# Forget-gate attention: half-row scores of two heads, token-major values, and an order written out for five engines

## The chip, the cores and the metric

The kernel runs on one core of a Trainium2 chip. The metric is the time on the device of one execution, in microseconds (us). Of the core's engines the text speaks of PE (TensorE: matmuls and transposes; its weight loads are recorded apart, as PEld), DVE (VectorE), ACT (ScalarE), POOL (GpSimd) and SP (SyncE, which issues most of the transfers).

## What is computed

The program is two transformer blocks over 1024 tokens of width 1024. All of the change lies in one layer of the first block, the forget-gate attention ("fox"): 16 heads of 64, a causal softmax over scores to which the difference of two cumulative log forget gates is added.

```python
def fox_layer(x, g_in, w_in, b_f, w_out):
    h = rms_norm(x, g_in)
    z = h @ w_in
    q, k, v, f_logit, gate = split_cols(z, ODD_SPLITS)     # 1024, 1024, 1024, 16, 1024
    log_f = jax.nn.log_sigmoid(f_logit.astype(jnp.float32) + b_f.astype(jnp.float32))
    log_cum = jnp.cumsum(log_f, axis=1)
    o = causal_block_attention(q.reshape(B, S, FOX_HEADS, FOX_HEAD_DIM), ..., log_cum=log_cum)
    return x + (o.reshape(B, S, FOX_WIDTH) * jax.nn.silu(gate)) @ w_out

# causal_block_attention, for each block of 128 queries:
        s = jnp.einsum('bqhd,bkhd->bhqk', qi, k) * scale
        s = s + ci[..., :, None] - lc_t[..., None, :]
        s = jnp.where(kpos[None, :] <= qpos[:, None], s, -jnp.inf)
        p = jax.nn.softmax(s, axis=-1)
        o = jnp.einsum('bhqk,bkhd->bqhd', p, v)
```

Products of single precision are made of three matmuls on operands that are split into a high and a low part (`mm3`: high by high, high by low, low by high).

## The kernel before

**Rounds.** The 16 heads are taken as 8 pairs p, and each pair runs over 8 query blocks i: 64 rounds n = 8p + i. In round n the scores are (i+1)·128 keys wide. `pipeline` with `FOX_SKEW = [2, 1, -2]` makes step t out of four things: scores and softmax of round t+2 (`soft`), the transposes of the probabilities of round t+1 (`tr`), the product with the values of round t-2 (`pv`), and `fill(t)`, which is one half of a projection of the next pair: 24 matmuls of 512 columns and their evacuation. Pairs 0 and 1 have three projections (q, k, gate), the pairs from 2 on also v: 8 units. In the last pair's steps `fill` runs units of a later stage (`k.mem.fill`) and loads for the layer's output projection (`ahead`).

**Scores.** For one head the high half of q stands on 64 partitions of a tile and the low half on the other 64, and the keys' high part (another tile: their low part) stands twice, on both halves. So a head's scores are two matmuls over all 128 rows (L595). The copies of the keys into the other half are 64 transfers of 128 KB issued by ACT (L1256, L1257), and q and k are evacuated by two instructions on 64 partitions for each part (L1245, L1246, L1254, L1255). DVE adds the bias and finds the row's bound (L600, two instructions or three for a head, the last one on the diagonal block with `dm` of L1309 on POOL), ACT makes the exponentials and their sum (L606), DVE the reciprocal (L608), POOL the scaling (L609).

**Transposes and values.** `tr` transposes up to four 128x128 blocks into one of two `pt` banks (L622), and ACT copies the bank out (L630): for i of 4 and more there are four such groups in a round, two for each head. `pv` multiplies with the values of the two heads, 64 output rows each, the heads one after the other (L644). The values of pairs 0 and 1 are made token by token ahead of the rounds (`V01`); those of the pairs from 2 on come out of a projection as features by tokens and are transposed back, 8 transposes for each pair (L1276) with two copies on DVE (L1277).

**Order.** In this stage SP alone issues in the source's order. PE, DVE, ACT and POOL are ordered by the scheduler, and the four generators of a step hand over to each other at each `yield`; a few order-only dependencies (`k.order`) keep transposes, products and projections of neighbouring rounds apart.

**Weights.** `plan` puts every weight piece on one list. `w_get` (used by `proj_units`) splits a piece into high and low (a cast on ACT, L316, a subtraction on DVE, L318) and also the next one on the list, one ahead, unless that one is marked `slot`.

PSUM has 8 banks here: two `pd` (projections), three `ps` (scores), two `pt` (transposes), one `po` (products).

## Time and profile before

| | us |
|---|---|
| median of three runs (lowest, highest) | 2300.29 (2298.59, 2302.42) |
| the profiled execution, its own time | 2301.81 |
| its span in the trace | 2300.0 |
| PE busy in the span | 2211.1 (96%) |
| rounds of the fox layer, 608.0 to 1203.2 | 595.2 |
| PE busy in them | 591.9 |
| DVE, ACT, POOL busy in them | 258.1, 274.6, 154.9 |

The page puts a core's engines side by side. The chain of waits follows the work that ended last back from the end of the program. A view by form groups instructions of one line and one shape with their mean duration; consecutive matmuls overlap in their records, so what one adds on PE is the distance between two starts, which the timeline gives. The view by windows gives each engine's busy time and the granted clock of PE in a stretch.

### The profile page before, as it was taken

The page shows a single profiled execution, that of the slowest core. Times are in us where ns is not written, and L with a number is a line of the kernel's source. Part 1 is how long each engine was busy: PE and PEld are TensorE (multiplying, and loading weights), DVE is VectorE, ACT ScalarE, POOL GpSimd, SP SyncE. Part 2 cuts the span into 40 slices and gives each one's busy share as a digit, 9 for nine tenths or more (in the row PEclk, how much of TensorE's full clock was granted, in tenths as well). Part 3 has the DMA queues.
Part 4 walks back from the last instruction along what each step waited for, and adds up shares of the span by engine and source line. Part 5 has one row for each costly group of instructions (what it writes and reads, how often), then busy time and mean ns, then how long its engine had stood idle before and what let it go on. Part 6 is the DMA issues. An engine that isn't in the chain of part 4 may idle for free.

```text
span 2300.0 us, 32867 instructions
## 1 busy us (share of the span) xinstructions
PE 2211.1 (96%) x12164; PEld 1757.5 (76%) x12164; DVE 1184.4 (51%) x2892; ACT 960.0 (42%) x2018; POOL 452.6 (20%) x620
## 2 busy tenths in 40 slices
PE   7999999999999999999999999999899999899797
PEld 7888778888877777777788789787577888666564
DVE  6322678834344443444344332687445637766544
ACT  5322667823344444444442221355202122557453
POOL 2000455400122222222310010121001102222121
PEclk9999999999999999999999999999999999999898
DMA  4112221233222211221254221326656124778774
GB/s 165 37 48 99 81 58 38 75 118 104 75 69 72 63 55 60 74 60 56 83 174 147 103 91 47 106 69 216 233 220 259 69 106 176 263 235 293 226 216 165
DMA packets 96515, 282.06 MB, mean 123 GB/s; under 512 B 11980, under 2 KB 25036, under 8 KB 96352
## 3 DMA queue, kind: packets, MB, share of 16 engines
q1 hardware_dynamic: 75616, 225.32, 28.4%
q0 software_dynamic: 6624, 24.12, 4.4%
q10 hardware_dynamic: 14112, 30.48, 4.2%
q8 instruction: 97, 1.59, 0.3%
q14 instruction: 66, 0.54, 0.1%
HBM read 202.73 MB, written 65.62 MB: 117 GB/s over the span
## 4 chain that ended last, share of the span: by engine, by line
PE 85%; DVE 6%; DMA 4%; ACT 3%; issue 2%; SPq 0%; POOL 0%; ACTq 0%; POOLq 0%; DVEq 0%
PE pd L340 15%; PE pd L342 15%; PE pd L341 15%; PE ps L340 4%; PE po L644 4%; PE ps L342 4%; PE ps L341 4%; PE ps L595 3%; PE pt L622 3%; PE pd L2538 2%; PE pd L1902 2%; PE ps L990 2%; PE po L1033 1%; PE pt L1019 1%; PE ps L2562 1%
## 5 line engine op out<-in xcount | busy, mean ns | idle before, releaser
L340 PE MATMUL pd<-fh,wh 128*128 128x512 f32 x880 | 353.5, 402 | 0.6 <-DVE st L1246 0.3
L342 PE MATMUL pd<-fh,wl 128*128 128x512 f32 x880 | 347.9, 395 | 0.5 <-DVE wl L318 0.5
L341 PE MATMUL pd<-fl,wh 128*128 128x512 f32 x880 | 347.4, 395 | 0.0
L340 PE MATMUL pd<-wh,fh 128*128 128x258 f32 (+3 forms) x616 | 203.2, 330 | 2.4 <-DVE n L1436 2.4
L342 PE MATMUL pd<-wh,fl 128*128 128x258 f32 (+3 forms) x616 | 200.9, 326 | 0.0
L341 PE MATMUL pd<-wl,fh 128*128 128x258 f32 (+3 forms) x616 | 200.8, 326 | 0.0
L340 PEld LDWEIGHTS pd<-fh,wh 128*128 128x128 f32 x880 | 165.2, 188 | 43.0 <-issue 7.1
L342 PEld LDWEIGHTS pd<-fh,wl 128*128 128x128 f32 x880 | 165.2, 188 | 40.1 <-issue 2.3
L341 PEld LDWEIGHTS pd<-fl,wh 128*128 128x128 f32 x880 | 165.5, 188 | 34.9 <-issue 0.2
L318 DVE TENSOR_TENSOR wl<-w,wh 128x1024 fp32r<-128x1024 f32 (+5 forms) x92 | 106.8, 1166 | 138.3 <-ACT wh L316 138.3
L316 ACT CAST wh<-w 128x1024 fp32r<-128x1024 f32 (+5 forms) x99 | 97.3, 989 | 139.3 <-PE pd L341 108.2
L630 ACT COPY PT<-pt 128x512 f32<-128x512 f32 (+2 forms) x192 | 86.4, 478 | 139.9 <-PE pt L622 139.4
L609 POOL TENSOR_SCALAR P<-P,rinv 128x256 f32<-128x256 f32 (+7 forms) x128 | 96.1, 751 | 192.3 <-DVE rinv L608 163.3
L606 ACT ACTIVATE P<-P,m 128x256 f32<-128x256 f32 (+7 forms) x128 | 99.6, 778 | 76.7 <-DVE m L600 75.8
L340 PEld LDWEIGHTS pd<-wh,fh 128*128 128x128 f32 x616 | 116.4, 189 | 14.2 <-DVE n L1436 2.8
L341 PEld LDWEIGHTS pd<-wl,fh 128*128 128x128 f32 x616 | 116.3, 189 | 10.6 <-issue 1.0
L342 PEld LDWEIGHTS pd<-wh,fl 128*128 128x128 f32 x616 | 116.3, 189 | 10.2 <-issue 0.2
L1309 POOL TENSOR_TENSOR dm<-lcb,mask 128x128 f32<-128x128 f32 x128 | 60.7, 474 | 282.4 <-DVE m L600 226.3
L595 PE MATMUL ps<-st,st 128*128 128x512 f32 (+3 forms) x384 | 106.9, 372 | 1.2 <-DMA st<-st 0.8
L644 PE MATMUL po<-PT,V 128*64 128x256 f32 (+1 forms) x640 | 96.4, 373 | 0.0
L2420 DVE TENSOR_TENSOR ml<-mw,mh 128x1024 fp32r<-128x1024 f32 x66 | 80.1, 1226 | 29.8 <-ACT mh L2417 15.4
L622 PE MATMUL pt<-ident,P 128*128 128x128 f32 x576 | 88.7, 276 | 2.6 <-POOL P L609 2.4
(513 smaller groups left out, 4721.9 us busy)
## 6 DMA issues: line engine op xcount, KB each, us to landing
mw<-w_moe SPq DMA_DIRECT2D x70, 512.0 KB
w<-o_wc SPq DMA_DIRECT2D x30, 512.0 KB
w<-w_moe SPq DMA_DIRECT2D x26, 512.0 KB
xr<-xs SPq DMA_DIRECT2D x18, 512.0 KB
s<-x_wkv SPq DMA_DIRECT2D x16, 512.0 KB
lcb<-dn SPq DMA_DIRECT2D x16, 512.0 KB
st<-st ACTq DMA_DIRECT2D x64, 128.0 KB
wkd<-kvw SPq DMA_DIRECT2D x32, 256.0 KB
```

The lines of the kernel that those rows point to most:

```text
L316: nc.scalar.copy(hi[:, :n], raw[:, :n])
L318: (eng or nc.vector).tensor_sub(lo[:, :n], raw[:, :n], hi[:, :n].bitcast(F32))
L340: first = mm(out, lhs[0], rhs[0], start=start, stop=False)
L341: mm(out, lhs[0], rhs[1], start=False, stop=False)
L342: mm(out, lhs[1], rhs[0], start=False, stop=stop)
L595: ins = nc.tensor.matmul(ps[:, :m], l, r, start=t == 0, stop=t == len(passes) - 1)
L606: nc.scalar.activation(sb[:, :w], sb[:, :w], AF.Exp, bias=acc, scale=-1.0, accum_out=sm)
L609: nc.gpsimd.tensor_scalar(sb[:, :w], sb[:, :w], ri, 0.0, op0=OP.mult, op1=OP.add)
L622: ins = nc.tensor.transpose(pt[:, j * 128:(j + 1) * 128], p[:, (c + j) * 128:(c + j + 1) * 128], k.ident)
L630: nc.scalar.copy(dst, src)
L644: st["V", n + i] = nc.tensor.matmul(o[a * 64:(a + 1) * 64, cols], val(a, j), PT[i // 2, a, j // 4][:, j % 4, n0:], start=j == 0, stop=j == ...
L2420: nc.vector.tensor_sub(W[c][1], raw[c], W[c][0].bitcast(F32))
```

## The change

The scores of both heads of a pair are made together. q and k are kept as four tiles (q high, q low, k high, k low), each with head 0 on partitions 0 to 63 and head 1 on 64 to 127; three matmuls for each head, over 64 rows each, alternate between the heads and go to separate banks. The copies of the keys go away, and each half of q or k is evacuated by one ACT and one DVE instruction on 128 partitions.

The values of two pairs (256 columns) are made token by token, in units of two token blocks: 48 matmuls 256 columns wide, 12 units for six pairs, at i = 6 and 7 of pairs 0 to 5. The transposes of the values go away. Their weights (`o_wv2`, two `slot` pieces for two pairs) stand in the list behind the pieces of pairs 1, 3 and 5, and are split in step i = 4 of pairs 0, 2 and 4.

The generators become plain functions, and all five engines issue in the source's order: `outs`, `score`, `turn`, `soft`, `fill` in each step.

```diff
+FOX_MAN = {ET.SP, ET.PE, ET.DVE, ET.Activation, ET.Pool}
...
+    A["o_wv2"] = np.stack([v[:, c * 256:(c + 1) * 256].reshape(8, 128, 256).transpose(1, 0, 2).reshape(128, 2048) for c in range(1, 4)])
...
-        ch += [q[:, c], kk[:, c]] + ([v[:, c]] if p >= 2 else []) + [gate[:, c]]
+        ch += [q[:, c], kk[:, c], gate[:, c]]
...
-def causal_attn(k, st, n, qk, bias, scale, val, done):
...
         def q_evac(half, ps):
...
-                nc.scalar.activation(q[r, cols], ps[r, :], AF.Copy, scale=0.125)
...
+            h, l = qk[p][:2]
+            nc.scalar.activation(h[:, cols], ps, AF.Copy, scale=0.125)
+            nc.vector.scalar_tensor_tensor(l[:, cols], ps, 0.125, h[:, cols].bitcast(F32), op0=OP.mult, op1=OP.subtract)
...
-                k.q.dma_start(out=h[o, cols].bitcast(F32), in_=h[r, cols].bitcast(F32))
-                k.q.dma_start(out=l[o, cols].bitcast(F32), in_=l[r, cols].bitcast(F32))
+            h, l = qk[p][2:]
+            nc.scalar.copy(h[:, cols], ps)
+            nc.vector.tensor_sub(l[:, cols], ps, h[:, cols].bitcast(F32))
...
+    def v_weights(g):
+        WV[g] = [k.w_get(i, 0) for i in k.fv2[g]]
+
+    def v_unit(g, x):
+
+        if x % 2 == 0:
+            V.setdefault(g, []).append(k.slot([128, 4, 256], name="V"))
+        ps = k.psd()
+        for t in range(2):
+            for kt in range(8):
+                wh, wl = WV[g][kt // 4]
+                c = slice(kt % 4 * 256, (kt % 4 + 1) * 256)
+                k.mm3(ps[:, t * 256:(t + 1) * 256], ft.stat(2 * x + t, kt), (wh[:, c], wl[:, c]), kt == 0, kt == 7)
+        nc.scalar.copy(V[g][x // 2][:, x % 2 * 2:x % 2 * 2 + 2, :].rearrange("p a b -> p (a b)"), ps)
...
+    def score(n):
+
+        p, i = divmod(n, 8)
+        w = (i + 1) * 128
+        qh, ql, kh, kl = qk[p]
+        ps = {}
+        for c in range(0, w, 512):
+            m = min(512, w - c)
+            for a in range(2):
+                ps[c, a] = k.psd() if c and a else k.pss()
+            for l, r in ((qh, kh), (qh, kl), (ql, kh)):
+                for a in range(2):
+                    h = slice(a * 64, a * 64 + 64)
+                    nc.tensor.matmul(ps[c, a][:, :m], l[h, i * 128:w], r[h, c:c + m], start=l is qh and r is kh, stop=l is ql)
...
+    def turn(n):
+        i, z = n % 8, n // 2
+        for a in range(2):
+            p = P.pop((n, a))
+            for c in range(0, i + 1, 4):
...
+                pt = k.pst()
+                for j in range(m):
+                    nc.tensor.transpose(pt[:, j * 128:(j + 1) * 128], p[:, (c + j) * 128:(c + j + 1) * 128], k.ident)
...
     def fill(t):
         p, i = divmod(t, 8)
...
         if i == 0:
             units[p] = prep(p + 1)
-        if i >= len(units[p]):
-            return []
...
+            g = p // 2 + 1
+            if p < 6:
+                units[p] += [lambda x=x: v_unit(g, x + p % 2 * 2) for x in range(2)]
+                if p % 2 == 0:
+                    units[p][4] = lambda u=units[p][4]: (u(), v_weights(g))
+        if i < len(units[p]):
             units[p][i]()
...
-    pipeline(64, [run(0), run(1), run(2)], FOX_SKEW, fill)
...
+    a, b, c = FOX_SKEW
+    with k.tc.manual_schedule(engines=FOX_MAN):
+        for t in range(-a, 64 - c):
+            if 0 <= t + c:
+                outs(t + c)
+            if t + a < 64:
+                score(t + a)
+            if 0 <= t + b < 64:
+                turn(t + b)
+            if t + a < 64:
+                soft(t + a)
+            if t < 64:
+                fill(t)
+            else:
+                weave([ahead(t - 56)])
...
+        k.fc.append([k.plan(A["o_wc"][p * 3 + j]) for j in range(3)])
+        if p in (1, 3, 5):
+            k.fv2[p // 2 + 1] = [k.plan(A["o_wv2"][p // 2, :, b * 1024:(b + 1) * 1024], 1024, True) for b in range(2)]
```

The next rows are PE's order before, at the transposes of block 5 of pair 3's first head (`pt` banks), with scores of block 6 (`ps`) and a projection (`pd`):

```order
L341 MATMUL pd_8801<-fl_5423,wh_8515 128x512
L342 MATMUL pd_8801<-fh_5422,wl_8516 128x512
L595 MATMUL ps_8755<-st_7657,st_7655 128x512 [waits DVE_49,PE_49]
L622 MATMUL pt_8693<-ident,P_8590 128x128 [waits Activation_49,Pool_49]
L622 MATMUL pt_8693<-ident,P_8590 128x128 x3
L622 MATMUL pt_8750<-ident,P_8590 128x128 [waits Activation_49]
L622 MATMUL pt_8750<-ident,P_8590 128x128
L595 MATMUL ps_8755<-st_7659,st_7655 128x512
L340 MATMUL pd_8801<-fh_5422,wh_8515 128x512
L595 MATMUL ps_8766<-st_7657,st_7655 128x384 [waits DVE_49]
L595 MATMUL ps_8766<-st_7659,st_7655 128x384
L341 MATMUL pd_8801<-fl_5423,wh_8515 128x512
```

The two groups of the second head follow 22 rows further down, behind the rest of that projection. The same place of the change, one block further (block 6 of pair 3, with the end of the scores ahead of it):

```order
L1230 MATMUL pd_8988<-qk_7823,qk_7821 128x512
L1230 MATMUL ps_8987<-qk_7823,qk_7822 128x512
L1230 MATMUL pd_8988<-qk_7823,qk_7822 128x512
L1265 MATMUL pt_9014<-ident,P_8890 128x128 [waits Pool_49]
L1265 MATMUL pt_9014<-ident,P_8890 128x128 x3
L1265 MATMUL pt_9021<-ident,P_8890 128x128 [waits Activation_49]
L1265 MATMUL pt_9021<-ident,P_8890 128x128 x2
L1265 MATMUL pt_9027<-ident,P_8899 128x128 [waits Activation_49,Pool_49]
L1265 MATMUL pt_9027<-ident,P_8899 128x128 x3
L1265 MATMUL pt_9034<-ident,P_8899 128x128 [waits Activation_49]
L1265 MATMUL pt_9034<-ident,P_8899 128x128 x2
L342 MATMUL pd_9049<-fh_5422,wh_8742 128x512 [waits DVE_49]
```

All four groups now stand together, on two banks, and the projection stands behind them.

The second place is the cast of the first weight piece of pair 4 (q), used first in step t = 24. ACT's order before (`wh_8193` is the piece; the P are probabilities of pair 2's blocks 6 and 7, `vT` a half of pair 3's values):

```order
L606 ACTIVATE P_7956,sum_8014<-P_7956,m_8012 128x896 [waits DVE_49]
L630 COPY PT_7865<-pt_7962 128x4x128 [waits PE_49]
L630 COPY PT_7921<-pt_8019 128x2x128 [waits PE_49]
L606 ACTIVATE P_8023,sum_8044<-P_8023,m_8042 128x896 [waits DVE_49]
L316 CAST wh_8193<-w_7788 128x1024 [waits DMAHW6_49,PE_49]
L1269 COPY vT_8003<-pd_8070 128x512 [waits PE_49]
L630 COPY PT_7931<-pt_8029 128x4x128 [waits PE_49]
L630 COPY PT_7952<-pt_8049 128x2x128 [waits PE_49]
L606 ACTIVATE P_8053,sum_8122<-P_8053,m_8120 128x1024 [waits DVE_49]
```

ACT's order of the change at the cast of the same piece (`wh_8562`), and below it PE's at its first use:

```order
L1209 COPY V_8367<-pd_8464 128x512
L1269 COPY PT_8446<-pt_8544 128x2x128
L1269 COPY PT_8450<-pt_8548 128x2x128
L1250 ACTIVATE P_8530,sum_8552<-P_8530,m_8535 128x384
L1250 ACTIVATE P_8537,sum_8557<-P_8537,m_8542 128x384
L318 CAST wh_8562<-w_8192 128x1024
L318 CAST wh_8568<-w_8198 128x1024
L1166 ACTIVATE qk_8599<-pd_8574 128x512
```

Before, the cast stands among the exponentials of pair 2, with 23 rows of ACT between it and the evacuation (L1245) of the bank that the piece first fills; in the change it stands behind the exponentials of the step that uses it, with one cast between it and that evacuation (L1166).

```order
L1230 MATMUL ps_8522<-qk_7823,qk_7822 128x384
L1230 MATMUL ps_8523<-qk_7823,qk_7822 128x384
L1265 MATMUL pt_8544<-ident,P_8432 128x128 [waits Pool_49]
L1265 MATMUL pt_8544<-ident,P_8432 128x128
L1265 MATMUL pt_8548<-ident,P_8439 128x128 [waits Pool_49]
L1265 MATMUL pt_8548<-ident,P_8439 128x128 [waits DVE_49]
L342 MATMUL pd_8574<-fh_5178,wh_8562 128x512 [waits Activation_49]
L343 MATMUL pd_8574<-fl_5179,wh_8562 128x512
L344 MATMUL pd_8574<-fh_5178,wl_8563 128x512 [waits DVE_49]
```

The step's projection now has a wait for ACT at its first row and one for DVE at its third, with nothing between the scores and it but four transposes.

## Rows read from the trace of the kernel before

**Rows 1.** The page: busy time of the engines, and the chain of waits by engine.

```profile
PE 2211.1 (96%) x12164; PEld 1757.5 (76%) x12164; DVE 1184.4 (51%) x2892; ACT 960.0 (42%) x2018; POOL 452.6 (20%) x620
...
PE 85%; DVE 6%; DMA 4%; ACT 3%; issue 2%; SPq 0%; POOL 0%; ACTq 0%; POOLq 0%; DVEq 0%
```

**Rows 2.** Windows: length, busy us of PE, PEld, DVE, ACT, POOL, granted clock, DMA.

```profile
608.00:1203.20 595.20, 591.91 (x3143) 451.54 (x3144) 258.11 (x846) 274.59 (x576) 154.91 (x253) 1.00 0.25 76
...
1142.90:1145.20 2.30, 1.35 (x8) 1.12 (x9) 1.42 (x7) 1.18 (x3) 1.16 (x2) 1.00 0.00 0
1145.20:1148.60 3.40, 3.40 (x15) 1.72 (x14) 1.36 (x7) 2.13 (x6) 1.62 (x3) 0.50 0.21 80
1435.90:1439.10 3.20, 0.00 (x1) 0.00 (x0) 1.07 (x6) 2.42 (x6) 0.00 (x0) 0.95 0.00 0
1439.10:1445.60 6.50, 5.92 (x23) 4.03 (x24) 2.33 (x6) 1.65 (x2) 0.00 (x0) 0.50 0.00 0
```

**Rows 3.** PE by form, 608.0 to 1203.2: busy us, mean ns of one, idle ahead.

```profile
L340 PE MATMUL pd<-fh,wh 128*128 128x512 f32 x448 | 180.1, 402 | 0.3 <-DVE st L1246 0.3
...
L622 PE MATMUL pt<-ident,P 128*128 128x128 f32 x576 | 88.7, 276 | 2.6 <-POOL P L609 2.4 <-ACT PT L630 0.2
L644 PE MATMUL po<-PT,V 128*64 128x256 f32 x512 | 82.6, 395 | 0.0
L595 PE MATMUL ps<-st,st 128*128 128x512 f32 x192 | 63.6, 421 | 0.3 <-DVE m L600 0.3
L1902 PE MATMUL pd<-s,s 128*128 128x256 f32 x128 | 28.9, 380 | 0.0
...
L1276 PE MATMUL pt<-ident,vT 128*128 128x128 f32 x48 | 7.2, 272 | 0.0
```

**Rows 4.** What PE waited for in the same stretch.

```profile
PE pt L622 <- POOL P L609: 2.4, 4, 0.9
PE ps L595 <- DMA st<-st: 0.8, 1, 0.8
```

**Rows 5.** Timeline, start and length: first and last of 16 matmuls in a row.

```profile
608.86 0.39 PE L341 MATMUL pd<-fl,wh 128*128 128x512 f32 x1
...
612.31 0.39 PE L341 MATMUL pd<-fl,wh 128*128 128x512 f32 x1
```

**Rows 6.** Timeline of PE around the product with the values.

```profile
765.50 0.62 PE L595 MATMUL ps<-st,st 128*128 128x384 f32 x2
766.05 1.95 PE L644 MATMUL po<-PT,V 128*64 128x256 f32 x16
767.93 0.50 PE L340 MATMUL pd<-fh,wh 128*128 128x512 f32 x1
```

**Rows 7.** Timeline of PE in a later stage, first and last of eight narrower matmuls.

```profile
1434.78 0.28 PE L341 MATMUL pd<-wl,fh 128*128 128x258 f32 x1
...
1435.63 0.28 PE L342 MATMUL pd<-wh,fl 128*128 128x258 f32 x1
```

**Rows 8.** Timeline: transposes, the copy of their banks, the next transposes.

```profile
1174.92 0.93 PE L622 MATMUL pt<-ident,P 128*128 128x128 f32 x7
...
1176.25 0.96 ACT L630 COPY PT<-pt 128x512 f32<-128x512 f32 x2
...
1176.97 0.96 PE L622 MATMUL pt<-ident,P 128*128 128x128 f32 x7 [0.20 <-ACT PT L630]
```

**Rows 9.** Timeline: first DVE and ACT instruction of block 2's softmax, one head.

```profile
765.59 0.42 DVE L600 CUSTOM_DVE_ANT_0 P<-ps,lcb 128x256 f32<-128x256 f32 x1
...
766.56 0.61 ACT L606 ACTIVATE P<-P,m 128x384 f32<-128x384 f32 x1 [0.64 <-DVE m L600]
```

**Rows 10.** ACT, then DVE, by form, 608.0 to 1203.2: splitting of weights, and copies.

```profile
L630 ACT COPY PT<-pt 128x512 f32<-128x512 f32 x96 | 54.6, 583 | 69.5 <-PE pt L622 69.1
L316 ACT CAST wh<-w 128x1024 fp32r<-128x1024 f32 x32 | 33.5, 1048 | 46.8 <-PE pd L341 43.8 <-DMA st<-st 2.9
...
L318 DVE TENSOR_TENSOR wl<-w,wh 128x1024 fp32r<-128x1024 f32 x31 | 38.8, 1251 | 42.1 <-ACT wh L316 42.1
```

More of the change, by code (lines that the diff above doesn't have):

```diff
@@ L1283, in g_evac @@
             k.silu2(gt[p][:, half * 512:(half + 1) * 512], ps)
-        ev = [q_evac, k_evac] + ([v_evac] if p >= 2 else []) + [g_evac]
         units = []
-        for e, i in zip(ev, k.fc[p]):
-            units += k.proj_units(ft, i, e, order=st.get(("V", (p - 1) * 8 - 1)))
+        for e, i in zip([q_evac, k_evac, g_evac], k.fc[p]):
+            units += k.proj_units(ft, i, e)
         if p == 0:
@@ new lines, in val @@
+    def val(p, a, j):
+        c = p % 2 * 128 + a * 64
+        return V[p // 2][j // 4][:, j % 4, c:c + 64]
+    def score(n):
[12 more added lines that the diff above has]
+        for a in range(2):
+            P[n, a] = k.slot([128, 1024], name="P")
+            dm = k.small([128, 128], "dm", bufs=3)
+            nc.gpsimd.tensor_add(dm, lcb[p][a][:, i * 128:w], k.mask)
+            M[n, a] = 1e30
+            for c in range(0, w, 512):
+                m = min(512, w - c)
+                for c0, c1, b in ((c, min(c + m, w - 128), lcb[p][a]), (w - 128, c + m, dm)):
+                    if c1 <= c0:
+                        continue
+                    mx = k.small([128, 1], "m", bufs=12)
+                    nc.vector.tensor_tensor_reduce(P[n, a][:, c0:c1], ps[c, a][:, c0 - c:c1 - c], b if b is dm else b[:, c0:c1],
+                                                   -1.0, M[n, a], OP.add, OP.min, mx)
+                    M[n, a] = mx
@@ new lines, in soft @@
+    def soft(n):
+        w = (n % 8 + 1) * 128
+        for a in range(2):
+            sb, sm = P[n, a], k.small([128, 1], "sum", bufs=8)
+            nc.scalar.activation(sb[:, :w], sb[:, :w], AF.Exp, bias=M.pop((n, a)), scale=-1.0, accum_out=sm)
+            ri = k.small([128, 1], "rinv", bufs=8)
+            nc.vector.reciprocal(ri, sm)
+            nc.gpsimd.tensor_scalar(sb[:, :w], sb[:, :w], ri, 0.0, op0=OP.mult, op1=OP.add)
+    def turn(n):
+        i, z = n % 8, n // 2
+        for a in range(2):
+            p = P.pop((n, a))
+            for c in range(0, i + 1, 4):
+                m, q = min(4, i + 1 - c), (z, a, c // 4)
+                if q not in PT:
+                    PT[q] = k.slot([128, 4, 256], name="PT")
+                pt = k.pst()
+                for j in range(m):
+                    nc.tensor.transpose(pt[:, j * 128:(j + 1) * 128], p[:, (c + j) * 128:(c + j + 1) * 128], k.ident)
+                dst = PT[q][:, :m, n % 2 * 128:(n % 2 + 1) * 128]
+                src = pt[:, :m * 128].rearrange("p (j n) -> p j n", j=m)
+                if (a + c // 4) % 4 < 3:
+                    nc.scalar.copy(dst, src)
+                else:
+                    nc.vector.tensor_copy(dst, src)
@@ new lines, in outs @@
+    def outs(n):
+        p, i = divmod(n, 8)
+        if i % 4 == 0:
+            po[0] = k.pso()
+        o, half = po[0], i // 2 + 1
+        last = half * 2 - 1
+        for j in range(i % 2 * half, (i % 2 + 1) * half):
+            n0 = 128 if j == last else 0
+            cols = slice((last - 1) % 4 * 128 + n0, (last % 4 + 1) * 128)
+            for a in range(2):
+                nc.tensor.matmul(o[a * 64:(a + 1) * 64, cols], val(p, a, j), PT[n // 2, a, j // 4][:, j % 4, n0:],
+                                 start=j == 0, stop=j == last)
+            if j % 4 == 3 or j == last:
+                for a in range(2):
+                    PT.pop((n // 2, a, j // 4))
+        if i % 4 == 3:
@@ L1321, in f @@
             t = k.slot([128, 512], name="go")
-            nc.vector.scalar_tensor_tensor(t, o, 0.5, gt[p][:, half * 512:(half + 1) * 512], op0=OP.mult, op1=OP.mult)
-            k.q.dma_start(out=god[p, :, half * 512:(half + 1) * 512], in_=t)
-        return f
+            cols = slice(i // 4 * 512, (i // 4 + 1) * 512)
+            nc.vector.scalar_tensor_tensor(t, o, 0.5, gt[p][:, cols], op0=OP.mult, op1=OP.mult)
+            k.q.dma_start(out=god[p, :, cols], in_=t)
     for u in prep(0):
         u()
-    stages = [causal_attn(k, st, p * 8, passes(p), bias(p), 1.0, val(p), done(p)) for p in range(8)]
@@ L1329, in fox @@
-    run = lambda s: (lambda n: stages[n // 8][s](n % 8))
     units = {}
```

142 lines of the change are left out of this document (12 added, 130 removed).

## The prediction, made before the change was run

> **What bounds the kernel now.** I read the page first: PE is busy for 96% of the span and carries 85% of the chain of waits, DVE 6%, the transfers 4%, ACT 3% [rows 1]. Then the windows: in the 595.2 us of the rounds PE is busy for 591.9, no other engine for half of that, at a granted clock of 1.00 [rows 2]. The waits of PE there add up to less than 4 us: four times for POOL's scaled probabilities, once for a copy of the keys [rows 4]. So the stage costs what PE issues, and every instruction or transfer that the change saves elsewhere (64 copies of keys, half of the q and k evacuations, 12 copies of values) lies beside PE and is worth nothing but the 0.8 us for which the first scores wait for a copy.
>
> To price PE's work I take distances between starts, since records overlap: 0.230 for 512 columns (15 steps in 3.45 us) [rows 5], 0.1215 for 256 (seven steps in 0.85) [rows 7], 0.109 for a transpose (seven records of 0.276 in 0.93) [rows 3, 8]; for scores of 128 columns I take 0.11 as for the transpose, for 384 the middle, 0.176. In the product with the values 16 records end in the time of eight passes: the two heads' records run side by side, about 0.22 a pass [rows 6].
>
> That gives the stage in us: 448 groups of three projection matmuls and 24 matmuls of the filler 314.6; scores 192·0.230 + 64·(0.176 + 0.1215 + 0.11) = 70.3; 624 transposes 68.0; 256 paired passes of the products at 0.22 and 64 narrow ones at 0.11 63.3; 128 records of another stage 27.6. The sum is 544, and 1.7 go to a short stretch at half clock. About 46 of the 591.9 us stay over. They sit at the products: one run goes from 765.50 to 767.93, 2.43 us for two scores (0.35) and eight passes (1.76), so 0.32 for getting in and out, 0.16 for each change of the array's mode [rows 6]. The scheduler cuts the products into some 100 runs, 0.46 us each; those longer ones hold one head alone, whose passes nothing runs beside.
>
> **The change part by part**, on PE unless said.
>
> *Values by token.* 12 units of 48·0.1215 = 5.8 us take the place of 12 of 24·0.230 = 5.5: +3.7. The 48 transposes go: -5.2.
>
> *Scores.* A pair costs 24·0.230 + 8·(0.176 + 0.1215 + 0.11) = 8.8 us now. After, it has 18 passes of 512 columns and six each of 384, 256 and 128, each pass two matmuls of 64 rows. No row of this trace shows two row halves at work; the nearest are the two column halves of the products, which share their passes, weight loads included [rows 6]. So I take the halves as running together: 18·0.230 + 6·0.4075 = 6.6, with a little for the second start 6.85. That is -1.94 for a pair, -15.5. The ends: one after the other, 13.2 a pair, +35; only the loads one after the other at the 0.11 of a transpose with its load [rows 8], 0.22 for each narrow pass, 8.1 a pair, -5.
>
> *The skill on this.* The Trainium skill, "TensorE: Matmul & The Clock Gate", Part 3, says that matmuls on different row groups run concurrently and that a weight load overlaps a running matmul only if the row group differs; it gives 3.07 times for four row tiles, not four. No run shows it here. If two tiles fell short in that proportion, as an estimate from that page, a pair's 6.85 would be 8.9 and the scores would save nothing; this is the second rival.
>
> *Modes.* All products of a round now stand in one run of both heads: 64 runs at 0.32, 20.5. But half-row scores are a mode of their own, between the products and the transposes, and leaving it may cost once more: 62·0.16 = 9.9. Together 30.4 for 46: -15.6. Bounds: -25 if leaving is free, -5 if it costs a full 0.32.
>
> *Transposes on two banks.* Here the change adds waits. From i = 4 on the four groups of a round stand together; the third needs the bank of the first, and behind it on PE wait the rest, the projection, and everything after. The first group's last record ends 0.276 after its start; the copy by ACT takes 0.583 [rows 10]; from the copy's end to the next transpose it is 0.14 (1176.25 + 0.58 to 1176.97) [rows 8]. Against that 1.0 PE has only the second group, i - 3 transposes, and the step itself: (i - 2)·0.109. So it stands for 0.78, 0.67, 0.56 and 0.45 us at i = 4 to 7: 2.46 a pair, 19.5 in all, a little less in the last pair, where the scheduler still puts output-projection matmuls between the groups. Before, scores and projections lay between the groups, and the same wait shows once, 0.2 us [rows 3, 8]. Where ACT serves at once this is a lower end; behind an evacuation it grows, up to 30.
>
> *Late weights.* The pieces of the values are marked `slot` and stand ahead of q of pairs 2, 4 and 6, so nothing splits q ahead, three times. PE's projection then waits for the cast, and ACT has the exponentials of the same step in front of it. After the scores (block 2): DVE 0.97 for a head, from 765.59 to 766.56, two heads 1.94; the second exponential 0.61 [rows 9]; the cast 1.05 [rows 10]; 0.14: 3.7 us, less four transposes, 3.3. The third matmul then needs DVE's 1.25 [rows 10], of which two matmuls cover 0.46: 0.8 more. 4.1 us, three times: +12.3. What waits behind it is all of PE, and the evacuations of that projection.
>
> *The clock.* After PE had stood still for over 3 us (1435.9 to 1439.1) the granted clock was 0.50, PE's lower level of 1.2 GHz, for 6.5 us, 5.9 of them busy: 3 lost; after two waits of 0.8 and 0.9 us inside 2.3 us it was 0.50 for 3.4 us: 1.7 lost [rows 2]. The late weights make three waits of the first size. I take 2.2 each: +6.6, between 0 and 9.
>
> *DVE, ACT, POOL, SP in the source's order.* A round's chain (bounds, exponentials, scaling) has a projection of 5.5 us, products and the next scores ahead of its transposes; by the rows above it needs about 4 to 7 us. I cost it at nothing; where there is no projection (two steps of pair 6) it could show, by under 1 us.
>
> Sum: +3.7 - 5.2 - 15.5 - 15.6 + 19.5 + 12.3 + 6.6 - 0.8 = +5.0 on the profiled execution's 2301.8: 2306.8. That execution lay 1.5 above the median, so 2305.3. The parts' own bounds, mostly independent, put this case between 2294 and 2318.
>
> **The rivals.**
>
> *Faster: modes are cheap and the clock holds.* If leaving the half-row scores costs nothing (transposes and projections follow each other at the plain distances today) and the three waits leave the clock alone, -9.9 - 6.6: 2289. For it: the half rows differ from full ones less than the products' column halves do. Against: the fall after 3 us is in the trace.
>
> *Slower: the halves share less.* The scores gain 5 us or nothing for 15.5: 2316 to 2321, say 2318. For it: no row shows them sharing. Against: the products' loads and passes do.
>
> *Slower: the halves don't share at all.* 13.2 a pair for 8.8: 2305.3 + 50.5 = 2356. It decides from the second pass on: starts of the two heads 0.23 apart at 512 columns.
>
> *Slower: the bank waits bring the clock down.* The stretch from 1142.9 to 1145.2 had PE busy for 1.35 of 2.30 us before the fall [rows 2]; the transposes of a round with i = 4 would be 1.1 of 1.9. If each of 32 such turns cost 1.7, 54 more: 2359. Against: long busy projections lie around each turn, while in that row the stage was running out.
>
> That the order isn't what the source says is ruled out but for the last two blocks, where it helps by about 1 us.
>
> **How the numbers follow.** The forecast has 0.45, the faster rival 0.24, partial sharing 0.13, no sharing 0.10, the clock at the turns 0.06, anything else 0.02. The forecast's own range gives 0.06 to faster, 0.19 to same, 0.20 to slower, and of the faster rival 0.21 lies below and 0.03 within. A measurement of this kernel tells about 0.2% (4.6 us) from no change. So faster 0.27, same 0.22, slower 0.51. For the range I leave out no sharing and the clock at the turns (0.16) and little else: 2283 to 2328. The likeliest alone is 2294 to 2318.
>
> **What would show it.** Of the changed kernel: by form, scores of 512 columns in pairs with starts a few ns apart (sharing) or 0.23 apart (none); in the list of waits, transposes waiting for ACT's copies some 32 to 64 times and about 20 us, and a projection waiting for a weight cast three times, over 3 us; by windows, 0.50 after those three or not; the products in 64 runs; POOL no longer waited for. The rounds should take about 600 us instead of 595. If the transposes' waits add up to under 10 us or the scores save under 10, the sum was wrong in those terms, whatever the total.

## The result, and the profile after

The changed kernel takes 2329.84 us (median of four runs, 2328.31 to 2335.10); the kernel before, on the same chip, 2299.86. The ratio is 1.0133, with a 95% interval of 1.0115 to 1.0151: 30 us slower. The sign was forecast as the likeliest, the size was not: 2305.3, and a range that ended at 2328.

PE still bounds the program; the page's first line of busy times, of the kernel after:

```profile
PE 2198.3 (94%) x12596; PEld 1753.8 (75%) x12596; DVE 1160.9 (50%) x2848; ACT 939.2 (40%) x1986; POOL 468.7 (20%) x620
```

The span grew by 27.5 us, from 2300.0 to 2327.5, while PE's busy time fell by 13 [rows 1]. Nearly all of that lies in the fox layer. The view by windows (columns as in [rows 2]) gives the rounds, from the first score to the last product, and inside them three waits of PE, each with the stretch at half clock (a granted clock of 0.50) that goes with it.

```profile
606.20:1225.70 619.50, 579.86 (x3589) 450.04 (x3588) 235.62 (x803) 253.84 (x544) 168.52 (x254) 0.97 0.18 60
...
853.80:857.00 3.20, 0.18 (x2) 0.11 (x1) 1.44 (x9) 3.00 (x8) 1.33 (x3) 0.78 0.00 0
855.60:862.40 6.80, 5.22 (x11) 3.67 (x12) 3.03 (x3) 2.19 (x4) 2.76 (x4) 0.50 0.35 109
...
822.10:824.70 2.60, 0.16 (x2) 0.10 (x2) 2.46 (x5) 0.80 (x2) 0.00 (x0) 1.00 0.72 189
824.90:828.30 3.40, 3.40 (x13) 2.92 (x12) 2.12 (x9) 2.71 (x5) 0.15 (x1) 0.50 0.71 233
...
1186.10:1192.20 6.10, 0.00 (x0) 0.03 (x1) 2.43 (x4) 1.39 (x2) 0.00 (x0) 0.83 0.49 166
1190.10:1196.90 6.80, 4.70 (x11) 3.76 (x12) 4.54 (x14) 0.97 (x2) 0.00 (x0) 0.50 0.57 174
```

There are six stretches at 0.50: three of 6.8 us behind the late weights (the one at 855.6 is shown), two of 3.4 (824.9 is shown), and the one at 1190.1. PE is busy for 27.3 us of them, so 13.7 are lost. That splits the rounds in three:

| us | before [rows 2] | after | difference | predicted |
|---|---|---|---|---|
| rounds | 595.2 | 619.5 | +24.3 | +5.0 |
| PE not busy | 3.3 | 39.6 | +36.3 | +31.0 |
| lost to half clock | 1.7 | 13.7 | +12.0 | +6.6 |
| the rest, PE's work | 590.2 | 566.2 | -24.0 | -32.6 |

The work after holds 36 matmuls of the output projection that the scheduler put ahead, 23 before (the prediction took them for the filler's), 3 us; without them it fell by 27. Ahead of the rounds 1.8 us went (the first score stands at 606.2, before at 608.0); behind them 5 came, two waits of 3.0 and 2.5 us and a stretch at half clock, less the 3 us of matmuls done earlier.

What PE waited for, from 600 to 1240 us:

```profile
PE pt L1265 <- ACT PT L1269: 21.4, 30, 2.5
PE pd L342 <- ACT wh L318: 9.1, 3, 3.0
PE ps L342 <- DVE m L1242: 6.1, 1, 6.1
PE ps L342 <- ACT fh L348: 3.0, 1, 3.0
PE pt L1265 <- POOL P L1253: 1.5, 4, 0.6
PE pd L344 <- DVE wl L320: 0.9, 3, 0.3
...
```

Before, the same list held 2.4 us for POOL and less than a microsecond for each of the others [rows 4]. The first two lines and the last shown are the two waits that the sum had: banks and late weights. The third it did not have, nor three of the 30 in the first line, of 2.5 us each. One of each of the expected ones in the timeline, PE at block 4 of a pair, and ACT and PE at the first q unit of the next:

```profile
884.39 0.77 PE L1265 MATMUL pt<-ident,P 128*128 128x128 f32 x5
885.87 0.73 PE L1265 MATMUL pt<-ident,P 128*128 128x128 f32 x5 [0.71 <-ACT PT L1269]
...
855.82 1.97 ACT L318 CAST wh<-w 128x1024 fp32r<-128x1024 f32 x2
...
856.89 0.80 PE L342 MATMUL pd<-fh,wh 128*128 128x512 f32 x1 [3.02 <-ACT wh L318]
...
858.40 0.80 PE L344 MATMUL pd<-fh,wl 128*128 128x512 f32 x1 [0.29 <-DVE wl L320]
```

The long ones have another cause. The trace, all engines, at the step of pair 0 that makes the scores of block 7 and the transposes of block 6 (the other two stand at the same step of pairs 2 and 4):

```profile
664.13 1.99 ACT L318 CAST wh<-w 128x1024 fp32r<-128x1024 f32 x2
...
665.20 2.36 DVE L320 TENSOR_TENSOR wl<-w,wh 128x1024 fp32r<-128x1024 f32 x2 [0.25 <-ACT wh L318]
...
665.86 0.98 PE L1265 MATMUL pt<-ident,P 128*128 128x128 f32 x7
...
667.48 0.68 DVE L1291 SCALAR_TENSOR_TENSOR go<-po,gt 128x512 f32<-128x512 f32 x1
...
668.20 0.34 ACTq L1292 DMA_DIRECT2D god<-go  x1
...
668.58 0.97 ACT L1269 COPY PT<-pt 128x512 f32<-128x512 f32 x2 [2.46 <-DVE go L1291]
...
669.31 0.95 PE L1265 MATMUL pt<-ident,P 128*128 128x128 f32 x7 [2.47 <-ACT PT L1269]
```

The two pieces of value weights are cast on ACT until 666.12. ACT's next instruction is not the copy of the bank: it is the issue of the store of a gated output (`god`), and that needs DVE's gating (L1291), which stands behind two weight subtractions. So the copies start at 668.58, and PE has waited 2.47. The list names ACT, but ACT itself had stood still since 666.12. Near the end the same happens with a transfer at the far end:

```profile
1184.48 0.37 SPq L1328 DMA_DIRECT2D gor<-god  x1
...
1188.55 1.04 ACT L348 CAST fh<-gor 128x1024 fp32r<-128x1024 f32 x1 [5.33 <-DMA gor<-god]
1189.62 1.23 DVE L349 TENSOR_TENSOR fl<-gor,fh 128x1024 fp32r<-128x1024 f32 x1 [5.17 <-ACT fh L348]
1190.77 0.68 DVE L1291 SCALAR_TENSOR_TENSOR go<-po,gt 128x512 f32<-128x512 f32 x1
...
1191.37 0.68 DVE L1242 CUSTOM_DVE_ANT_0 P<-ps,lcb 128x512 f32<-128x512 f32 x1
...
1192.20 0.77 PE L342 MATMUL ps<-wh,fh 128*128 128x512 f32 x1 [6.15 <-DVE m L1242]
```

ACT and DVE both stand at the split of an input of the output projection whose load was issued at 1184.48. The bounds of scores that were finished at 1185 come six microseconds late behind it, and PE waits for their bank.

That the row halves run together is plain in PE's timeline; the two heads go to `ps` and `pd`:

```profile
1184.51 0.40 PE L1230 MATMUL ps<-qk,qk 64*128 64x512 f32 x1
1184.51 0.40 PE L1230 MATMUL pd<-qk,qk 64*128 64x512 f32 x1
1184.74 0.39 PE L1230 MATMUL ps<-qk,qk 64*128 64x512 f32 x1
1184.75 0.39 PE L1230 MATMUL pd<-qk,qk 64*128 64x512 f32 x1
```

Both start within 0.01 us, and the next pass 0.23 later, the pitch of a single 512-column matmul [rows 5]. Pairs of 256 columns follow each other at 0.12 (883.94, 884.06 and 884.18 in the same trace), so the narrow passes share their loads too.

### The profile page after: what moved, and what is told of

Read it like the earlier page. It is cut to its first block, busy times and chain, and to the rows that moved or that the text cites. A ratio compares the mean times of both kernels' runs of the same rounds, so it can differ in the third digit from the quotient of the medians.

```text
span 2327.5 us, 33431 instructions
## 1 busy us (share of the span) xinstructions
PE 2198.3 (94%) x12596; PEld 1753.8 (75%) x12596; DVE 1160.9 (50%) x2848; ACT 939.2 (40%) x1986; POOL 468.7 (20%) x620
## 5 line engine op out<-in xcount | busy, mean ns | idle before, releaser
L343 PE MATMUL pd<-fl,wh 128*128 128x512 f32 x784 | 311.7, 398 | 0.0
L342 PE MATMUL pd<-wh,fh 128*128 128x256 f32 (+3 forms) x808 | 257.6, 319 | 2.2 <-DVE n L1417 1.9
L344 PE MATMUL pd<-wh,fl 128*128 128x256 f32 (+3 forms) x808 | 255.1, 316 | 0.0
L343 PE MATMUL pd<-wl,fh 128*128 128x256 f32 (+3 forms) x808 | 254.5, 315 | 0.0
L342 PEld LDWEIGHTS pd<-wh,fh 128*128 128x128 f32 x808 | 152.3, 189 | 14.1 <-DVE n L1417 2.7
L343 PEld LDWEIGHTS pd<-wl,fh 128*128 128x128 f32 x808 | 152.4, 189 | 10.6 <-issue 1.0
L344 PEld LDWEIGHTS pd<-wh,fl 128*128 128x128 f32 x808 | 152.2, 188 | 10.2 <-issue 0.2
L1242 DVE CUSTOM_DVE_ANT_0 P<-ps,lcb 128x512 f32<-128x512 f32 (+3 forms) x112 | 64.1, 573 | 86.4 <-PE ps L1230 85.4
L342 PE MATMUL ps<-wh,fh 128*128 128x512 f32 (+1 forms) x216 | 83.4, 386 | 14.0 <-DVE m L1242 6.1
L1265 PEld LDWEIGHTS pt<-ident,P 128*128 128x128 f32 x576 | 62.0, 141 | 44.3 <-issue 36.9
```

The source lines that it names most:

```text
L342: first = mm(out, lhs[0], rhs[0], start=start, stop=False)
L343: mm(out, lhs[0], rhs[1], start=False, stop=False)
L344: mm(out, lhs[1], rhs[0], start=False, stop=stop)
L1242: nc.vector.tensor_tensor_reduce(P[n, a][:, c0:c1], ps[c, a][:, c0 - c:c1 - c], b if b is dm else b[:, c0:c1], -1.0, M[n, a], OP.add, OP.m ...
L1265: nc.tensor.transpose(pt[:, j * 128:(j + 1) * 128], p[:, (c + j) * 128:(c + j + 1) * 128], k.ident)
```

## The experiments

The theory: PE's work fell, and the written-out order gave back more than that in waits and in the clock behind them. Its rivals: the new computation is no cheaper; or each wait, once removed, turns up elsewhere.

| kernel | median, us | ratio to before, 95% interval |
|---|---|---|
| the change | 2329.8 | 1.0133 (1.0115 to 1.0151) |
| q split one step ahead | 2311.6 | 1.0047 (1.0030 to 1.0063) |
| store issued by SP | 2330.7 | 1.0140 (1.0123 to 1.0157) |
| heads' transposes apart | 2322.6 | 1.0105 (1.0083 to 1.0126) |
| the scheduler's order | 2304.9 | 1.0030 (1.0018 to 1.0042) |
| heads' passes one after the other | 2329.2 | one run |
| loads near the end earlier | 2320.8 | 1.0106 (1.0089 to 1.0123) |
| gating later | 2319.2 | 1.0095 (1.0078 to 1.0112) |
| the four repairs together | 2283.9 | 0.9933 (0.9917 to 0.9950) |
| the same, heads' transposes together | 2290.4 | 0.9963 (0.9949 to 0.9978) |
| the four, head 0's transposes first | 2286.6 | 0.9954 (0.9940 to 0.9968) |
| the same but for block 7 | 2277.5 | 0.9906 (0.9893 to 0.9920) |

**Late weights.**

```diff
         if i < len(units[p]):
             units[p][i]()
+        if i == 7 and p in (0, 2, 4):
+            k.w_split(k.wsp + 1)
```

> The changed kernel with one addition: behind the last unit of steps 7, 23 and 39 the next q piece is split, one step ahead of its use. Theory (the waits of the written-out order and the clock that they bring down are what the change lost): the three waits of a projection for its weight cast (3.02 us, and 0.30 for the subtraction) go, and so do the three stretches of 6.8 us at half clock behind them (3.4 us each): -20 us, about 2310. Rival (the cast isn't what is late; the projection would wait for the step's evacuations anyway): the wait stays under another name and less than 5 us are gained.

2311.6, 18 us faster than the change: as the theory had it. No wait for `wh` or `wl` is left in the list. The rounds took 601.9 us instead of 619.5, and half clock cost 6.7 us in them instead of 13.7:

```profile
606.40:1208.30 601.90, 571.98 (x3589) 446.15 (x3588) 234.84 (x803) 253.91 (x544) 168.12 (x254) 0.99 0.18 61
```

**The store of the gated outputs.**

```diff
-            k.q.dma_start(out=god[p, :, cols], in_=t)
+            nc.sync.dma_start(out=god[p, :, cols], in_=t)
```

> The changed kernel, with the stores of the gated outputs issued by SP instead of ACT. In the trace of the changed kernel the copies of a transpose bank wait 2.4 us in ACT's queue at three places, behind two weight casts and behind the issue of such a store, which itself waits for DVE's gating behind two weight subtractions. Theory (the store's issue holds ACT): the three waits of 2.45 us fall to the 0.33 to 0.44 of the same block elsewhere and the half clock behind them (3.4 us, 1.7 lost) goes: -11 us, about 2319. Rival (the two casts hold ACT as long): the waits stay at 2 us and more, and the time within 3 us of 2330.

2330.7: by time the rival, by the trace the theory. At the same place as above the wait is now short, with the gating as late as before:

```profile
667.76 0.96 PE L1265 MATMUL pt<-ident,P 128*128 128x128 f32 x7 [0.44 <-ACT PT L1269]
667.96 0.68 DVE L1291 SCALAR_TENSOR_TENSOR go<-po,gt 128x512 f32<-128x512 f32 x1
```

So the casts were not what held ACT. But now SP stands at the store, and its loads behind it. In the change SP issues a load of the filler (`x_wkv`) at 1140.07, 20 us ahead of the filler's matmuls at 1160.33; here it issues the store at 1147.30, when the gating ends, and that load only at 1148.68, for matmuls at 1156.22. So near the end the filler waits for it, and half clock goes with that (the list of waits, then a window).

```profile
PE pd L1883 <- DMA s<-x_wkv: 4.2, 1, 4.2
```

```profile
1154.20:1161.00 6.80, 4.78 (x11) 3.87 (x12) 1.43 (x2) 1.03 (x3) 3.04 (x4) 0.50 0.66 234
```

Moving the waiting instruction to another queue moved the cost. The next run moves what it waits for.

**The gating later.** `outs` only notes what is to be gated; a function behind the transposes does the gating and issues the store on ACT.

```diff
             if 0 <= t + b < 64:
                 turn(t + b)
+            gated()
             if t + a < 64:
                 soft(t + a)
```

> The changed kernel with the gating of an output and its store placed behind the step's transposes and scores instead of ahead of them; ACT still issues the store. Theory (the store's issue, waiting for DVE behind two weight subtractions, holds the bank copies; with the store on SP the waits went but SP's loads near the end paid for it): the three waits of 2.45 us fall to about 0.4 and the half clock behind them goes, and nothing is paid elsewhere: -11 us, about 2319. Rival (the gating put later frees the products' single bank later, and the next products wait): within 4 us of 2330, with products waiting for DVE.

2319.2, the theory's number, but not all of it for the theory's reason. The longest wait for a bank copy is 0.7 us, as it had it, and one wait of 2.1 for the gating appears, near the end. The half clock did not go, though. The rounds of the profiled execution (2316.0 us):

```profile
606.80:1221.70 614.90, 579.59 (x3589) 450.38 (x3588) 236.28 (x803) 254.23 (x544) 168.15 (x254) 0.98 0.18 60
```

They lose 13.7 us to half clock, as in the change: two stretches of 3.4 us stand elsewhere, one at 623.6 and one with the wait of 2.1. So the rounds are only 4.7 us shorter. The rest of this execution's lead lies behind them (1092.5 us for 1101.8), spread over stages that the edit leaves alone; that part is luck.

**The end.** What is loaded goes on a list and is split when the next step begins.

```diff
-                    t = k.xslot([128, 2, 512], name="gor")
+                    t = k.slot([128, 2, 512], name="gor")
                     nc.sync.dma_start(out=t, in_=god[2 * j:2 * j + 2, ...
-                    hi, lo = go.piece(hf, j)
-                    k.split(hi, lo, t)
+                    G.append((hf, j, t))
...
```

> The changed kernel; the inputs of the output projection are loaded into the large pool instead of the one of three, both halves at once, and split one step after their load. Theory (near the end ACT and DVE stand at a cast whose transfer could only start when the half before it had been split, and the transposes' copies and the scores' bounds stand behind it): the 6.15 us wait at the filler's bank and the half clock behind it (3.4 us lost) go, the waits of 3.0 and 2.5 us in the output projection may shrink: -8 to -15 us, 2315 to 2322. Rival (those transfers are late whatever holds them, or the wait turns up at the next cast): less than 4 us.

2320.8, 9 us: the wait of 6.1 us is gone from the list, and of the two behind the rounds the one of 3.0 fell to 1.6 and the one of 2.5 is gone. The half clock in the rounds did not shrink with them (14.0 us lost in the profiled execution).

**The transposes of the two heads apart.**

```diff
+            if 0 <= t + b < 64:
+                turn(t + b, [0])
             if t + a < 64:
                 score(t + a)
             if 0 <= t + b < 64:
-                turn(t + b)
+                turn(t + b, [1])
```

> The changed kernel with the transposes of a round cut in two: head 0's ahead of the step's scores, head 1's behind them, on the same two banks. Theory (the third group waits only because the copy of the first has not ended): the plain waits of 0.33 to 0.71 us, 15.6 us in all, go under the scores' 0.5 to 1.6 us; the three long ones shrink by the scores' time: -16 to -25 us, 2305 to 2314. Rival (the probabilities come just in time): head 0's transposes then wait for POOL by 0.3 to 1 us in each round, and the time stays at 2325 to 2340.

2322.6: 7 us instead of 16 or more. The plain bank waits went, as the list shows (5 waits for copies are left of 30), but at the start and in the last steps, where no projection lies ahead, head 0's transposes come before POOL is done:

```profile
PE pt L1265 <- ACT PT L1269: 14.9, 5, 7.2
...
PE pt L1265 <- POOL P L1253: 6.5, 5, 2.7
```

The three long waits stay at 2.5: what holds them is the store's issue, which has nothing to do with the banks. The wait at the end grew to 7.2, and two for POOL are new: 2.7 at the start and 2.3 at 1154.4. The expectation that they would shrink was wrong.

**The four together** (transposes apart in steps 2 to 53 alone), then **without the transposes apart**:

> The changed kernel with all four: q split one step ahead, head 0's transposes ahead of the scores (in steps 2 to 53 alone, where a projection lies ahead of them), the gating behind the transposes, the loads near the end as in the run before this. Theory (the new computation takes 26 us off PE's work and the waits and the clock are what ate it): 18 for the late weights, 11 for the gating, 12 to 15 for the bank waits, 8 to 15 near the end: 2270 to 2282, faster than the kernel before. Rival (the waits taken away come back at the next queue): 2290 or more.

> The kernel with all four repairs but one: both heads' transposes stand together behind the scores again, four groups on two banks. It prices the bank waits without the side effects that cutting them had in the changed kernel. Theory: 28 waits of 0.33 to 0.71 us come back in the pairs with a projection beside them, 14 us, too short to bring the clock down: 2296 to 2300, about as the kernel before. Rival (the copies' delay was partly that of the other three repairs): less than 8 us slower than with all four.

2283.9: 2 us above the theory's 2270 to 2282, below the rival's lower limit of 2290, and 15 us faster than the kernel before. Alone the four gave 18, 11, 9 and 7 us, 45 in all; together they gave 46, so what one of them takes away does not come back at the next. The rounds by windows, and from the list of PE's waits the line for the banks:

```profile
606.70:1180.70 574.00, 567.30 (x3572) 440.48 (x3571) 233.96 (x803) 259.06 (x544) 166.97 (x254) 0.99 0.19 63
```

```profile
PE pt L1265 <- ACT PT L1269: 2.1, 4, 0.7
```

With the heads' transposes together there are 30 such waits again, 15.9 us (the same two views):

```profile
606.70:1189.30 582.60, 562.79 (x3572) 439.84 (x3571) 234.95 (x803) 254.47 (x544) 166.86 (x254) 1.00 0.19 63
```

```profile
PE pt L1265 <- ACT PT L1269: 15.9, 30, 0.7
```

Yet the time is only 6.5 us longer, which is the rival's number: PE stands still for 19.8 us instead of 6.7, but is busy for 4.5 less, 3.0 of it work (the rest is half clock), which fits that a step has one change of mode less with the transposes in one place. The waits themselves are those that the theory had; what it left out is that price.

**The modes.** Two runs put head 0's transposes ahead of the products, next to the projection; the first in all of steps 2 to 53, the second, shown here, with the exception of block 7.

```diff
+            if first and t % 8 != 6:
+                turn(t + b, first)
             if 0 <= t + c:
                 outs(t + c)
-            if first:
+            if first and t % 8 == 6:
                 turn(t + b, first)
```

> The kernel with all four repairs, head 0's transposes put ahead of the products with the values instead of between them and the scores (steps 2 to 53). A step then changes the array's mode three times (transposes to products, products to scores, scores to transposes) instead of four. Theory (each change costs about 0.2 us whatever lies on its sides): 52 changes fewer, -8 to -11 us, 2272 to 2277, and PE's work in the rounds 553 to 556 us instead of 564. Rival (the probabilities of head 0 aren't ready that early, or a change is hidden): transposes wait for POOL, or the work stays at 562 or more, and the time at 2281 or more.

> The kernel of the run before, with head 0's transposes ahead of the products in every step but those of block 7 (t = 8p + 6), where they stand between the products and the scores. In the run before POOL's probabilities of block 7 came 0.5 to 1.9 us after the transposes wanted them, six times, and the half clock followed twice. Theory (a change of mode less is worth its 0.15 us wherever POOL is in time): the 7 us of waits go, PE's work stays at 557 to 559: 2276 to 2280, faster than the kernel with the four repairs. Rival (the waits move to the next block): 2283 or more.

The first came out at 2286.6, no faster than the four repairs: by time the rival. Its PE was busy for 562.2 us of the rounds instead of 567.3, and without what half clock cost for 557.2 instead of 564.1, close to the theory's 553 to 556; but POOL was late for block 7 (windows, then waits):

```profile
607.70:1182.90 575.20, 562.20 (x3572) 442.62 (x3571) 233.32 (x803) 255.56 (x544) 167.00 (x254) 0.99 0.19 64
```

```profile
PE pt L1265 <- POOL P L1253: 8.2, 9, 1.9
```

The second, without that block, took 2277.5 us, as the theory had it, and 0.9906 of the kernel before; it beats both kernels (windows, then waits).

```profile
605.90:1173.00 567.10, 560.28 (x3572) 442.97 (x3571) 233.63 (x803) 255.41 (x544) 167.04 (x254) 0.99 0.20 64
```

```profile
PE pt L1265 <- POOL P L1253: 2.0, 5, 0.6
```

Both it and the four repairs have two stretches of 3.4 us at half clock in their rounds, so the busy times compare: 567.3 - 560.3 = 7.0 us for 46 changes of mode fewer, 0.15 each. The Trainium skill, "TensorEngine Tiling (Array Packing)", Key Properties, says that changing the tiling mode drains the engine. The traces agree that a change costs time, 0.15 us here; what the engine does in that time they do not show.

The rounds of this kernel are 28 us shorter than before (567.1 for 595.2), its profiled execution only 22: behind the rounds it takes 8 us more (1105.2 for 1096.8). In the first 100 us there PE waits for 5.6 us, mostly until ACT and DVE have split the inputs of the output projection and of the next stage, and loses 1.7 to half clock; before, it did neither there.

**The scheduler's order.**

```diff
-FOX_MAN = {ET.SP, ET.PE, ET.DVE, ET.Activation, ET.Pool}
+FOX_MAN = {ET.SP}
```

> The changed kernel with one line changed: only SP follows the source in this stage, the four other engines are ordered by the scheduler as in the kernel before. It tells the new computation from the new order. Theory (PE's work became about 33 us cheaper, the order's waits and clock took 60): the waits go, some of the gain is cut into more runs of products and scores: 2270 to 2290, faster than the kernel before. Rival (half-row scores and values by token are no cheaper, and the order costs little): 2310 to 2330.

2304.9, between the two. The waits went, as the theory had it, but so did most of the gain. The view by line of these rounds, against the same lines of the change:

```profile
L1283 PE MATMUL po<-PT,V 128*64 128x256 f32 (+1 forms) x640 | 87.7, 381 | 4.4 <-DVE go L1291 4.4
...
L1230 PE MATMUL ps<-qk,qk 64*128 64x512 f32 (+3 forms) x480 | 77.1, 377 | 0.6 <-DVE m L1242 0.6
```

```profile
L1283 PE MATMUL po<-PT,V 128*64 128x256 f32 (+1 forms) x640 | 76.2, 368 | 0.0
L1230 PE MATMUL ps<-qk,qk 64*128 64x512 f32 (+3 forms) x480 | 69.9, 373 | 0.5 <-DVE m L1242 0.5
```

The same instructions are busy for 18.7 us longer. Some 5 of these are half clock: the profiled execution, the slowest of ten (2313.0 us), has two stretches of 6.8 us at 0.50 near the end of the rounds, and 10.6 us of these instructions lie in them. The rest goes with the order. The scheduler cuts products and scores into 71 and 80 runs and puts 105 runs of transposes and 102 of projections between them, and only 275 passes of the products and 246 of the scores start as pairs of the two heads; in the change it is 63, 65, 67 and 65 runs, and 320 and 283 pairs. So the order earns what it then wastes in waits. The theory's 2270 to 2290 had left that out.

**Half rows alone.** The order in which the two heads' passes are issued, and then full rows in their place, in the kernel with the four repairs:

```diff
-            for l, r in ((qh, kh), (qh, kl), (ql, kh)):
-                for a in range(2):
+            for a in range(2):
+                for l, r in ((qh, kh), (qh, kl), (ql, kh)):
```

> The changed kernel with the scores' matmuls in another order: three passes of head 0, then three of head 1, in place of head by head in turns. Theory (two row halves share their time only if their matmuls stand next to each other): PE's work in the rounds grows by 30 to 40 us, starts lie 0.23 us apart at 512 columns, about 2360 to 2370. Rival (what got cheaper is not the sharing but the number of runs): within 8 us of 2330.

```diff
-            for l, r in ((qh, kh), (qh, kl), (ql, kh)):
-                for a in range(2):
-                    h = slice(a * 64, a * 64 + 64)
-                    nc.tensor.matmul(ps[c, a][:, :m], l[h, i * 128:w], r[h, c:c + m], ...
+            for a in range(2):
+                for r in (kh, kl):
+                    nc.tensor.matmul(ps[c, a][:, :m], qh[:, i * 128:w], r[:, c:c + m], ...
```

> The kernel with all four repairs, its scores made of full rows again: for each head two matmuls over all 128 rows (q high by k high, q high by k low) in place of three over 64. The scores are not the reference's, since each matmul sums over both heads and the third pass is left out; everything else stays. It prices half rows alone, in a written-out order. Theory (half rows save 6.6 for 8.8 us a pair but leave a mode of their own, 8.1 measured with that in the changed kernel, so little is left): 3 to 8 us slower than with half rows, 2287 to 2292. Rival (the halves' sharing is what the change lives on, as the 15.5 us of the prediction): 12 us slower or more, 2296.

The first run left the time where it was (2329.2). Against the theory's wording the halves share their time although three matmuls of one head are issued ahead of the other's three; at 384 columns, `pd` behind `ps`:

```profile
893.79 0.33 PE L1230 MATMUL pd<-qk,qk 64*128 64x384 f32 x1
893.96 0.34 PE L1230 MATMUL ps<-qk,qk 64*128 64x384 f32 x1
893.97 0.34 PE L1230 MATMUL pd<-qk,qk 64*128 64x384 f32 x1
```

The first `pd` pass, fourth in the issue, runs ahead of the last two of `ps`. So that run could not take the sharing away, and its rival isn't shown either. The second did take it away. Its total (2879.9 us) says nothing: the wrong scores change what the last stage is given, whose work depends on it. The rounds can be read:

```profile
605.60:1173.40 567.80, 561.92 (x3380) 452.94 (x3378) 233.94 (x803) 257.73 (x544) 166.92 (x254) 1.00 0.19 64
```

PE is busy for 561.9 us at full clock, against 567.3 less 3.2 lost at half clock with half rows. So full rows are 2 us cheaper in that order (one execution of each), where scores lie between two groups of transposes and half rows change the mode twice. Added up from start to start, with waits and half clock left out, half rows take 65.6 us for the scores instead of 76.1, and 71.6 for the transposes beside them instead of 59.4. Both expectations had half rows ahead.

## Why the prediction missed

**What PE does: right, if 6 us too large.** The parts summed to -32.6, the rounds show -24.0, or -27 without the output projection's matmuls. The choice that the halves run together held, with loads and all; the range's other end, +35, and the partial sharing that the Trainium skill's 3.07 of four would mean ("TensorE: Matmul & The Clock Gate", Part 3) are not in the trace, which has a pair of passes in the time of one. The rule on loads that the prediction cites beside it does not fit the traces: in the projections, which use all rows, the load of the next matmul lies wholly under the running one (0.19 us from 658.09 in the trace of the change, under a matmul from 658.09 to 658.49). The change of mode at 0.16 held where it was measured best (0.15). What the sum did not say is that the two nearly cancel: 15.5 for half rows less 9.9 for leaving them was to be a gain of 5.6 in this order; with two changes a step it was a loss of 2. By parts, added up from start to start in the two traces with waits and half clock left out, projections and values with their transposes went from 323.5 to 322.0 us, the 1.5 of the sum; scores from 86.4 to 65.8, products from 88.7 to 71.8 and the transposes of the probabilities from 58.4 to 69.8, 26.1 together where the sum had 31.1.

**The waits on two banks: right.** 0.78 to 0.45 us were forecast for blocks 4 to 7; 0.71, 0.55, 0.44 and 0.33 came, 15.9 us for all in the run that has them alone, for 19.5.

**Late weights: right.** 4.1 us each were forecast, 3.3 measured, three times; with the clock 18 us, by the run without them.

**The clock: too small.** 6.6 for 12.0. The three stretches cost 2.6 each (5.2 busy of 6.8 us at 0.50), not 2.2, and 5.7 came behind waits that the sum did not have. The rival in which every bank wait brings the clock down didn't happen: no stretch at half clock follows one of the 0.3 to 0.7 us. Part of what the clock costs in one execution is chance, though. Three waits of 0.51, 0.56 and 0.35 us at 620 to 623, the last 0.24 in one run, stand in the change and in eight of the other runs; 3.4 us at half clock follow them in five of these nine, and not in the change.

**The step that failed** is the one that cost DVE, ACT, POOL and SP in the source's order at nothing. It followed one round's chain from scores to probabilities and found it short enough. It did not follow each queue row by row across the other things in it: the store's issue on ACT behind DVE's gating, the gating behind the weight subtractions of the values, the loads near the end behind a pool of three tiles. These are the three waits of 2.5 us, the one of 6.15 and the two behind the rounds, 19 us, and some 7 of lost clock: 26 against a miss of 24.5. The two runs that remove only these gained 11 and 9. They show the waits to come from these queues; the 7 us of clock are put down to them by place alone, since in the rounds of both runs half clock cost as much as in the change. The other misses nearly cancel: less gained on PE's work, less lost to the banks and to late weights.

The range fell short by 2 us because no rival held a queue: each of them was a price of PE or of its clock.

What stays open: how the 26.1 us of scores, products and transposes divide between half rows and the fewer runs was not measured in the change's own order. Full rows with the reference's scores were not tried in the written-out order; they need two more tiles a pair and the copies of the keys, and whether they would beat 2277.5 is not known.

## What to carry to other kernels

When an order is written out for all engines, walk each queue, not only the chain of the work: for every instruction that waits, the issues of stores and loads included, ask what stands behind it on its engine and who needs that. Grouping work by the array's mode paid 0.06 to 0.15 us here for each change fewer. A wait that the grouping opens costs its length, and where the clock falls with it, about two thirds as much again (13.7 us with 21 us of such waits). Put the waiting instruction behind the work that does not need it, rather than on another queue.

## What the runs showed of the hardware

- Matmuls on the two row halves ran together even when three of one half were issued ahead of the other's three: the starts lay 0.01 us apart, and pairs of 512, 384 and 256 columns followed each other at 0.23, 0.17 and 0.12 us.
- A change of the array's mode cost 0.15 us over 46 changes fewer (transposes moved from between products and scores to ahead of the products), and 0.06 over 52 fewer (head 0's transposes moved from ahead of the scores to behind them), so its price is not one number.
- In the change the granted clock fell to 0.50, the lower level of 1.2 GHz, for 3.4 us with two of three waits of 2.5 us and for 6.8 us with each of three waits of 3.0 us; in three other runs it was 3.4 us at the first of those three. Bank waits of 0.7 us and less, thirty in the run that has them alone, did not bring it down once; three waits of 0.51, 0.56 and 0.35 us within three microseconds did in some executions.
